# A decoder layer on one core: half of a gated mixer one product earlier, constants behind the input on another queue, row vectors in high and low parts

## The chip, the cores and the metric

The kernel runs on one core of one Trainium2 chip. A core has TensorE (PE, matrix products), VectorE (DVE), ScalarE (ACT), GpSimd (POOL), and SyncE (SP), which here only issues DMAs. Times are microseconds (us) of the device for one execution; the number that counts is the median over runs of the same kernel. [...]

## The reference

One decoder layer on a sequence of 1024 tokens of width 1024, fp32:

```python
proj = x @ w_in + b_in
u, v, c_q, c_kv, k_rope_raw, gate_gm, gate_mla = jnp.split(proj, IN_SPLITS, axis=-1)
y_gm = gmlp_branch(gelu(u), gelu(v), gm_ln_g, gm_ln_b, gm_w_s, gm_b_s) @ w_gm_out   # u * (tril(W_s) LN(v)_chunk + b)
y_mla = mla_branch(c_q, c_kv, k_rope_raw, positions, ...) @ w_mla_out                # 16 heads, causal
merged = sigmoid(gate_gm) * y_gm + sigmoid(gate_mla) * y_mla
x = layer_norm(DEEPNORM_ALPHA * x + merged @ w_o, ln1_g, ln1_b)
x = layer_norm(DEEPNORM_ALPHA * x + memory_cross_attention(x, mem, w_mq, w_mk, w_mv, w_mo), ln2_g, ln2_b)
y_moe = hierarchical_moe(x, ...)                                                     # top-1 group, top-2 experts
return layer_norm(DEEPNORM_ALPHA * x + y_moe, ln3_g, ln3_b)
```

The gated mixer (gMLP) works in chunks of 128 tokens with 8 channel groups; the two halves of the sequence (4 chunks each) are computed one after the other. The latent attention (MLA) has 16 heads. The memory attention has 256 memory tokens and 4 heads.

## The kernel before

**Products in three passes.** Every fp32 operand is split into a rounded high part (fp32r) and a remainder (`split`, L108: the high part by ACT, the low part by DVE), and a product is three fp32r matmuls, high by high, high by low and low by high (`mm3`, L125 to L127, and `proj_t`, L380 to L384). A weight tile goes through `load_w` (L114): SP loads it (L118), ACT and DVE split it, PE reads it. There are 3 raw buffers and 5 split ones, so the loads run several products ahead.

**What sets the order.** Outside the hand-ordered stages (the attention sweep, router and experts) the framework's scheduler puts the instructions on each engine in an order that it works out from the program and from tile buffers; the program text decides who waits on whom, and a stage written earlier is usually issued earlier. Each engine then runs its list in order and waits at an instruction whose input is missing. `defer(n, f)` in the program puts an action n products later.

**Start.** `latents` (L220) loads x, transposed, in eight tiles of 128 x 1024 (512 KB each), and the q-latent weights in four. `late_consts` (L205) follows in the text, six small DMAs on SP's queue (biases, norm gains, rope table).

**Input projection.** `proj_in_t` (L311) is one product of x with 128 of the columns: 24 steps of two matmuls of 128 x 512, then ACT's gelu or sigmoid into `to` and a store. Products 8 to 15 are one gate (`gg_d`), 16 to 23 the other (`gm_d`); 0 to 7 are u. v is made by `proj_v` and stored in `v_d`.

**gMLP.** `gmlp(half)` (L674) reads four chunks of v (`vl`, SP L698), normalises each by two DVE instructions (L699, L700) and splits them into `vs`. It returns `step(g)`: one group's product of `wsT` and `vs` (L704, by mm3), ACT's bias, a load of u, and one product later `turn` (L713): PE transposes, DVE multiplies, SP stores `a_d`. There are eight steps per half, two for each product of the loop in `build` (L1710 to L1723). After the last step `load_a` (L737) loads the eight 512 KB tiles of `a_d` into `aT` and splits them.

**Gated product and MLA.** `gate_gm` (L744) makes eight products of `aT` with `w_gmo` (24 steps of two matmuls each) and, between them, runs the first steps of the attention, which loads per head (`load`, L478): `kr_d` and `kn_d` into `kT` (32 and 64 partitions), `qn_d` and `qr_d` into `qT` (64 and twice 16 partitions), `vv_d` into `vT`. `kT`, `qT` and `vT` lie where x's tiles were, so these loads cannot start before x's last product (23) has ended.

**Memory keys.** `mem_kv` (L634) makes eight products (f = 0 to 7), each 24 matmuls of 128 x 256. Beside them `factors` (L762) turns the attention's row sums into factors by way of GpSimd's queue (`sum_d`, `rinv_d`, `fac`), and `scale_o` (L789) spreads them by two matmuls (L798) a tile. `next(scale)` (L658) places the first of them after f = 5 and the second after f = 7.

**Experts and the end.** The expert stage runs in pairs numbered i; PE is its bound and ACT and DVE split the weights (`wh`, `wl`). From i = 20 `final_loads` (L1557) brings the two vectors of the last norm, each of 1024, on one partition, and spreads them over 128 partitions by fp32 matmuls with a row of ones (L1570). `final` (L1573) norms eight tiles of 128 tokens, the last instruction of each an L1623 on DVE for tiles 5 to 7, and stores them (L1624).

Of the kernel before, what the change touches and what calls it, by code (L numbers as in the profile page):

```python
# [13 lines left out]
F32 = mybir.dt.float32  # L14
FR = mybir.dt.float32r
# [3 lines left out]
ALU = mybir.AluOpType  # L19
# [47 lines left out]
ALL = slice(0, 1024)  # L67
# [7 lines left out]
class K:  # L75
# [126 lines left out]
        self.ones = p.tile([128, 128], FR, name="ones")  # L202
        ts(self.ones, jp, 0.0, 1.0, op0=ALU.mult, op1=ALU.add)

    def late_consts(self):  # L205
        self.router_consts()
        for t, n in ((self.bt, "b_t"), (self.gq, "g_q"), (self.gkv, "g_kv"), (self.bs, "b_s"), (self.fr, "rope_c"), (self.rb, "b_r")):
            self.nc.sync.dma_start(t, self.i[n])

    def natural(self, ps, t, x, w, kts=range(8), nk=8):  # L210

# [8 lines left out]
    def latents(self, xT, fill):  # L220

        nc = self.nc
        with ExitStack() as px:
            small = px.enter_context(self.pool("p1small", 2))
            pss = [self.bank() for _ in range(8)]
            wt = None
            for kk in range(4):
                for kt in (2 * kk, 2 * kk + 1):
                    raw = self.gp.tile([128, 1024], F32, name="xraw", tag="g")
                    nc.sync.dma_start(raw, self.i["xT"][kt])  # L230
                    self.split(xT.at(0, kt, ALL), xT.at(1, kt, ALL), raw)
                    if kt % 2 == 0:
                        wt = self.load_w(self.i["w_cq"][kk], 768)
                for kt in (2 * kk, 2 * kk + 1):
                    o = (kt % 2) * 384
                    for t in range(8):
                        self.natural(pss[t][:, :384], t, xT, lambda k: (wt[:, 0, o:o + 384], wt[:, 1, o:o + 384]), [kt])
                    self.unit()
            self.late_consts()
            bcq = small.tile([128, 384], F32, name="bcq", bufs=1)  # L240
            self.bcast(bcq, self.i["b_cq"])
            bkv = small.tile([128, 320], F32, name="bkv", bufs=1)
# [391 lines left out]
    def mem_kv(self, px):  # L634

        nc = self.nc
        mt = [p.tile([128, 2048], FR, name="memT", tag="act").rearrange("p (k n) -> p k n", k=8) for p in self.pa]
        for k in range(2):
            self.split(mt[0][:, 4 * k:4 * k + 4], mt[1][:, 4 * k:4 * k + 4], self.memr[:, k])
        px.close()  # L640
        self.oT = Act(self.pb, "oT")
        fac = self.factors(px)
        next(fac)
        scale = self.scale_o()
        for f in range(8):
            w = self.load_w(self.i["w_mk"][f], 1024)
            ps = self.bank()
            for kt in range(8):
                self.mm3(ps[:, :256], *w128(w)(kt), mt[0][:, kt], mt[1][:, kt], kt == 0, kt == 7)
            st = self.gp.tile([128, 1024], F32, name="mkst", tag="g").rearrange("p (a n) -> p a n", a=4)  # L650
            self.split(st[:, 0].bitcast(FR), st[:, 1], ps[:, :256])
            self.unit()
            self.defer(1, lambda f=f, st=st: nc.sync.dma_start(self.mk_d[f], st[:, 0:2]))
            self.load_o(f)
            if f == 0:
                next(fac, None)
            if f in (5, 7):
                next(scale)  # L658
        for sl in range(2):
            wts = [self.load_w(self.i["w_mv"][sl, kk], 1024) for kk in range(4)]  # L660
            for m in range(2):
                ps = self.bank()
                ms = slice(m * 128, (m + 1) * 128)
                for kt in range(8):
                    self.mm3(ps, mt[0][:, kt, ms], mt[1][:, kt, ms], *w512(wts)(kt), kt == 0, kt == 7)
                st = self.gp.tile([128, 1024], F32, name="mvst", tag="g").rearrange("p (a n) -> p a n", a=2)
                self.split(st[:, 0].bitcast(FR), st[:, 1], ps)
                self.unit()
                self.defer(1, lambda m=m, sl=sl, st=st: nc.sync.dma_start(self.mv_d[m, :, :, sl * 512:(sl + 1) * 512], st))
                next(scale)  # L670
        for _ in scale:
            pass
# [774 lines left out]
    def experts(self, rest, xg):  # L1447
        nc, tc = self.nc, self.tc
# [8 lines left out]
        for i in range(NP):  # L1457
# [33 lines left out]
                sel = self.select(gi[:, NP - 1:])  # L1491
            if i == 24:
                self.nb = nc.values_load(self.nbi[0:1, 0:1], min_val=0, max_val=15)
            if i in (22, 24):
                next(lgb, None)
            if i == NP - 1:
                self.flush()
# [59 lines left out]
    def final_loads(self, px):  # L1557
        nc = self.nc
        self.lgb = px.enter_context(self.pool("lgb", side="right")).tile([128, 2, 1024], F32, name="lgb")
        self.fin = px.enter_context(self.pool("fins", 8, side="right"))  # L1560
        one = self.fin.tile([1, 128], F32, name="one", bufs=1)
        nc.gpsimd.memset(one, 1.0)
        for j, n in enumerate(("ln3_g", "ln3_b")):
            row = self.fin.tile([1, 1024], F32, name="row", bufs=1)
            nc.sync.dma_start(row, self.i[n])
            yield
            for q in range(2):
                c = slice(q * 512, (q + 1) * 512)
                pg = self.bank_g()
                nc.tensor.matmul(pg, one, row[:, c], start=True, stop=True)  # L1570
                nc.scalar.activation(self.lgb[:, j, c], pg, AF.Copy)  # L1571

    def final(self, first=True):  # L1573

        nc, mm = self.nc, self.nc.tensor.matmul
# [15 lines left out]
        def row_sum(t):  # L1591
# [27 lines left out]
            if t < 5:  # L1619
                nc.scalar.activation(u, u, AF.Copy, scale=r)  # L1620
                nc.gpsimd.tensor_tensor(u, u, lb, op=ALU.add)
            else:
                stt(u, u, r, lb, op0=ALU.mult, op1=ALU.add)  # L1623
            nc.sync.dma_start(self.out[t], u)  # L1624

        rows = [row_sum(t) for t in range(8)]
        for t in range(9):
# [16 lines left out]
def build(nc, tc, ctx, ins, out, upto=99):  # L1644
# [25 lines left out]
    with ExitStack() as dense:  # L1670
# [5 lines left out]
        with ExitStack() as late, ExitStack() as mla, ExitStack() as front:  # L1676
                k.psp = front.enter_context(k.pool("psd1", 8, PSUM))
                with ExitStack() as px:
# [19 lines left out]
                    with ExitStack() as gm:  # L1698
                        k.g1 = gm.enter_context(k.pool("g1"))
                        k.gsm = gm.enter_context(k.pool("gsm", 2))  # L1700
                        k.proj_v(xT)
                        k.proj_in_t(xT, 8)
                        st = k.gmlp(0)
                        k.proj_in_t(xT, 9)
                        k.proj_in_t(xT, 10)
                        for j in range(4):
                            st(2 * j)
                            k.proj_in_t(xT, 11 + j)
                            st(2 * j + 1)
                        k.proj_in_t(xT, 15)  # L1710
                        st = k.gmlp(1)
                        k.proj_in_t(xT, 16)
                        k.proj_in_t(xT, 17)
                        for j in range(4):
                            st(2 * j)
                            k.proj_in_t(xT, 18 + j)
                            st(2 * j + 1)
                        k.proj_in_t(xT, 22)
                        k.flush()
                    w = k.load_w(k.i["w_t"][23], 1024)  # L1720
                    aT = Act(front.enter_context(k.pool("aT", 8, side="right")), "aT")
                    k.load_a(aT)
                    k.proj_in_t(xT, 23, w)  # L1723
                    k.flush()
                k.mem_load(late)
                k.mla_pools(mla)
# [50 lines left out]
    n = 0  # L1777
# [128 lines left out]
```

## Time and profile before

| | |
|---|---|
| median of 3 runs | 2033.64 us (2032.84 to 2034.22) |
| the profiled execution's own time | 2035.97 us |
| its span | 2034.2 us |
| mean granted clock of TensorE | 0.985 |
| PE busy | 1977.6 us, 97% of the span |
| DVE busy | 1292.5 us, 64% |
| ACT busy | 1003.3 us, 49% |
| POOL busy | 449.2 us, 22% |
| chain that ended last | PE 91%, DMA 3%, DVE 3%, ACT 1%, issue 1% |
| DMA | 457.29 MB, mean 225 GB/s |

PE's share of busy time counts a matmul at the low clock as busy for twice as long, so time is lost in two ways: PE idle, and PE busy at a granted clock of 0.50. A row of the timeline gives start, duration, engine, line, operation, tiles and, in brackets, the idle time just before it and what ended that. A row of a DMA issue (SPq) says when SP issued it and how long that took, not when the data landed.

### The profile page before, as it was taken

The page shows a single profiled execution, that of the slowest core. Times are in us where ns is not written, and L with a number is a line of the kernel's source. Part 1 is how long each engine was busy: PE and PEld are TensorE (multiplying, and loading weights), DVE is VectorE, ACT ScalarE, POOL GpSimd, SP SyncE. Part 2 cuts the span into 40 slices and gives each one's busy share as a digit, 9 for nine tenths or more (in the row PEclk, how much of TensorE's full clock was granted, in tenths as well). Part 3 has the DMA queues.
Part 4 walks back from the last instruction along what each step waited for, and adds up shares of the span by engine and source line. Part 5 has one row for each costly group of instructions (what it writes and reads, how often), then busy time and mean ns, then how long its engine had stood idle before and what let it go on. Part 6 is the DMA issues. An engine that isn't in the chain of part 4 may idle for free.

```text
span 2034.2 us, 25602 instructions
## 1 busy us (share of the span) xinstructions
PE 1977.6 (97%) x9468; PEld 1630.4 (80%) x9468; DVE 1292.5 (64%) x2040; ACT 1003.3 (49%) x1267; POOL 449.2 (22%) x243
## 2 busy tenths in 40 slices
PE   8999999999999999999999999997999999999996
PEld 8888888888787777777888888886788888888884
DVE  5636533441335888857436516477888888888887
ACT  4432422322304777764212315233777777777774
POOL 0002000000100111110001100022545555557752
PEclk9999999999999999999999999997999999999998
DMA  5154963353783555537535712555899999999966
GB/s 184 54 210 155 382 196 134 143 189 136 245 251 104 126 125 125 125 133 239 184 106 180 268 62 73 161 218 231 286 372 381 381 387 396 401 392 369 377 260 250
DMA packets 147897, 457.29 MB, mean 225 GB/s; under 512 B 18077, under 2 KB 64029, under 8 KB 118744
## 3 DMA queue, kind: packets, MB, share of 16 engines
q1 hardware_dynamic: 138040, 438.58, 61.7%
q0 software_dynamic: 9728, 17.03, 2.2%
q8 instruction: 76, 1.25, 0.2%
q14 instruction: 53, 0.43, 0.1%
HBM read 367.10 MB, written 104.79 MB: 232 GB/s over the span
## 4 chain that ended last, share of the span: by engine, by line
PE 91%; DMA 3%; DVE 3%; ACT 1%; issue 1%; SPq 0%; POOL 0%; POOLq 0%; ACTq 0%
PE bank L125 9%; PE bank L126 9%; PE bank L127 9%; PE py L1355 8%; PE bank L380 8%; PE bank L382 8%; PE bank L384 8%; PE pg L125 6%; PE pg L127 5%; PE pg L126 5%; PE po L564 2%; PE po L566 2%; PE po L565 2%; PE st L538 1%; PE st L540 1%; PE st L542 1%
## 5 line engine op out<-in xcount | busy, mean ns | idle before, releaser
L1426 ACT ACTIVATE wh<-raw 128x2048 fp32r<-128x2048 f32 (+1 forms) x198 | 361.1, 1859 | 36.3 <-issue 31.4
L1435 DVE TENSOR_TENSOR wl<-raw,wh 128x2048 fp32r<-128x2048 f32 (+1 forms) x166 | 363.3, 2236 | 4.6 <-PE pg L126 3.0
L1435 POOL TENSOR_TENSOR wl<-raw,wh 128x2048 fp32r<-128x2048 f32 x32 | 202.9, 6340 | 227.6 <-ACT wh L1426 227.6
L110 ACT ACTIVATE wsp<-wraw 128x1024 fp32r<-128x1024 f32 (+5 forms) x118 | 111.6, 947 | 263.7 <-PE bank L384 155.2
L125 PE MATMUL pg<-wh,ex 128*128 128x512 f32 x512 | 203.4, 397 | 0.7 <-ACT ex L110 0.7
L126 PE MATMUL pg<-wl,ex 128*128 128x512 f32 x512 | 200.0, 391 | 2.0 <-DVE wl L1435 2.0
L127 PE MATMUL pg<-wh,ex 128*128 128x512 f32 x512 | 200.6, 392 | 0.0
L111 DVE TENSOR_TENSOR wsp<-wraw,wsp 128x1024 fp32r<-128x1024 f32 (+5 forms) x118 | 127.6, 1083 | 96.2 <-ACT wsp L110 93.7
L1355 PE MATMUL py<-wh,ehs 128*128 128x512 f32 x512 | 143.7, 402 | 2.9 <-DVE ehs L111 2.4
L380 PE MATMUL bank<-xT,wsp 128*128 128x512 f32 x384 | 120.1, 390 | 0.0
L382 PE MATMUL bank<-xT,wsp 128*128 128x512 f32 x384 | 119.9, 390 | 0.0
L384 PE MATMUL bank<-xT,wsp 128*128 128x512 f32 x384 | 119.7, 390 | 0.0
L735 POOL TENSOR_TENSOR xr<-xr,lb 128x1024 f32<-128x1024 f32 x12 | 28.7, 2395 | 409.4 <-ACT xr L734 409.4
L546 ACT ACTIVATE pe<-st 128x768 f32<-128x768 f32 (+5 forms) x128 | 86.3, 674 | 59.6 <-DVE st L544 59.5
L126 PEld LDWEIGHTS pg<-wl,ex 128*128 128x128 f32 x512 | 96.7, 189 | 21.3 <-DVE wl L1435 2.3
L125 PEld LDWEIGHTS pg<-wh,ex 128*128 128x128 f32 x512 | 96.4, 188 | 21.1 <-ACT lgb L1571 1.5
L127 PEld LDWEIGHTS pg<-wh,ex 128*128 128x128 f32 x512 | 96.5, 189 | 20.6
L1355 PEld LDWEIGHTS py<-wh,ehs 128*128 128x128 f32 x512 | 91.3, 189 | 19.4 <-DVE ehs L111 3.1
L125 PE MATMUL bank<-wsp,xT 128*128 128x512 f32 (+2 forms) x256 | 91.2, 363 | 6.5 <-ACT wsp L110 6.5
L319 ACT ACTIVATE to<-bank,cols 128x512 f32<-128x512 f32 x48 | 30.4, 684 | 133.7 <-PE bank L384 133.7
L548 ACT ACTIVATE pq<-pe 128x768 fp32r<-128x768 f32 (+5 forms) x128 | 91.3, 713 | 4.1
L126 PE MATMUL bank<-wsp,xT 128*128 128x512 f32 (+2 forms) x256 | 91.6, 358 | 0.0
(410 smaller groups left out, 4627.4 us busy)
## 6 DMA issues: line engine op xcount, KB each, us to landing
raw<-w_gu SPq DMA_DIRECT2D x124, 1024.0 KB
raw<-w_dn SPq DMA_DIRECT2D x62, 1024.0 KB
wraw<-w_t SPq DMA_DIRECT2D x24, 512.0 KB
kn_d<-st SPq DMA_DIRECT2D x8, 1024.0 KB
qn_d<-st SPq DMA_DIRECT2D x8, 1024.0 KB
vv_d<-vt SPq DMA_DIRECT2D x16, 512.0 KB
qT<-qn_d SPq DMA_DIRECT2D x16, 512.0 KB
kT<-kn_d SPq DMA_DIRECT2D x16, 512.0 KB
```

The lines of the kernel that those rows point to most:

```text
L110: a = nc.scalar.activation(hi, src, AF.Copy)
L111: (lo_eng or nc.vector).tensor_tensor(lo, src, hi.bitcast(F32), op=ALU.subtract)
L125: mm(out, ah, bh, start=start, stop=False)
L126: mm(out, ah, bl, start=False, stop=False)
L127: mm(out, al, bh, start=False, stop=stop)
L380: mm(ps, wh, x.at(0, kt, h), start=st, stop=False)
L382: mm(ps, wh, x.at(1, kt, h), start=False, stop=False)
L384: mm(ps, wl, x.at(0, kt, h), start=False, stop=sp)
L548: nc.scalar.activation(pq[:, 0, q0:], e[:, q0:], AF.Copy)
L1355: self.nc.tensor.matmul(py[:, q * 512:(q + 1) * 512], hs[:, a, js], w[b][:, j * 1024 + q * 512:j * 1024 + (q + 1) * 512], start=start and ...
L1426: self.nc.scalar.activation(w[0][:, c], self.raws[n][:, c], AF.Copy)
L1435: eng.tensor_tensor(w[1][:, c], self.raws[n][:, c], w[0][:, c].bitcast(F32), op=ALU.subtract)
```

## The change

The change has six parts.

- **Start.** The first x tile and the first weight tile are loaded and split in two halves each (512 and 384 columns), in turn. The six constants are issued by GpSimd instead of SP, and wait there for the ACT instruction that splits the last x tile.
- **gMLP.** `gmlp(1)` is called ahead of product 15 instead of behind it, and its steps stand one product earlier: the first two around product 17 instead of 18.
- **aT.** With that `load_a` stands ahead of product 22 instead of 23.
- **Memory keys.** The first `next(scale)` comes after f = 6 instead of f = 5.
- **Last norm's vectors.** They are loaded in four pieces of 512 straight into row 0 of their final tile, split into high and low on one partition, and spread by two fp32r matmuls each with ones; the pieces are worked on in pairs 21 to 28 instead of 22 and 24.
- **End.** The last L1623 and its store go in two halves of 512 columns.

```diff
-    def late_consts(self):
+    def late_consts(self, behind):
         self.router_consts()
         for t, n in ((self.bt, "b_t"), (self.gq, "g_q"), (self.gkv, "g_kv"), (self.bs, "b_s"), (self.fr, "rope_c"), (self.rb, "b_r")):
-            self.nc.sync.dma_start(t, self.i[n])
+            d = self.nc.gpsimd.dma_start(t, self.i[n])
+            self.tc.add_manual_dep(d.ins, behind.ins.name, mybir.DependencyInfo(mybir.DependencyClass.Sync, mybir.DependencyReason.DATA), reason="behind larger transfers")
...
+                    if kt == 0:
+                        wraw = self.rawp.tile([128, 1024], F32, name="wraw", tag="wraw")
+                        wt = self.wp.tile([128, 2, 1024], FR, name="wsp", tag="wsp")
+                        cs = [(slice(512 * j, 512 * j + 512), slice(384 * j, 384 * j + 384)) for j in range(2)]
+                        for c, cw in cs:
+                            nc.sync.dma_start(raw[:, c], self.i["xT"][kt][:, c])
+                            nc.sync.dma_start(wraw[:, cw], self.i["w_cq"][kk][:, cw])
+                        for c, cw in cs:
+                            self.split(xT.at(0, kt, c), xT.at(1, kt, c), raw[:, c])
+                            self.split(wt[:, 0, cw], wt[:, 1, cw], wraw[:, cw])
+                        continue
...
-            if f in (5, 7):
+            if f in (6, 7):
                 next(scale)
...
-            if i in (22, 24):
+            if 21 <= i <= 28:
                 next(lgb, None)
...
-        one = self.fin.tile([1, 128], F32, name="one", bufs=1)
-        nc.gpsimd.memset(one, 1.0)
         for j, n in enumerate(("ln3_g", "ln3_b")):
-            row = self.fin.tile([1, 1024], F32, name="row", bufs=1)
-            nc.sync.dma_start(row, self.i[n])
-            yield
             for q in range(2):
                 c = slice(q * 512, (q + 1) * 512)
+                high, low = (self.fin.tile([1, 512], FR, name=m, bufs=1) for m in ("high", "low"))
+                row = self.lgb[:1, j, c]
+                nc.sync.dma_start(row, self.i[n][:, c])
+                yield
+                self.split(high, low, row)
+                yield
                 pg = self.bank_g()
-                nc.tensor.matmul(pg, one, row[:, c], start=True, stop=True)
+                nc.tensor.matmul(pg, self.ones[:1], high, start=True, stop=False)
+                nc.tensor.matmul(pg, self.ones[:1], low, start=False, stop=True)
                 nc.scalar.activation(self.lgb[:, j, c], pg, AF.Copy)
...
-                stt(u, u, r, lb, op0=ALU.mult, op1=ALU.add)
-            nc.sync.dma_start(self.out[t], u)
+                for c in halves if t == 7 else [slice(0, 1024)]:
+                    stt(u[:, c], u[:, c], r, lb[:, c], op0=ALU.mult, op1=ALU.add)
+                    if t == 7:
+                        nc.sync.dma_start(self.out[t][:, c], u[:, c])
+            if t < 7:
+                nc.sync.dma_start(self.out[t], u)
...
+                        st = k.gmlp(1)
                         k.proj_in_t(xT, 15)
-                        st = k.gmlp(1)
                         k.proj_in_t(xT, 16)
-                        k.proj_in_t(xT, 17)
                         for j in range(4):
                             st(2 * j)
-                            k.proj_in_t(xT, 18 + j)
+                            k.proj_in_t(xT, 17 + j)
                             st(2 * j + 1)
-                        k.proj_in_t(xT, 22)
+                        k.proj_in_t(xT, 21)
                         k.flush()
-                    w = k.load_w(k.i["w_t"][23], 1024)
+                    w = k.load_w(k.i["w_t"][22], 1024)
                     aT = Act(front.enter_context(k.pool("aT", 8, side="right")), "aT")
                     k.load_a(aT)
-                    k.proj_in_t(xT, 23, w)
+                    k.proj_in_t(xT, 22, w)
+                    k.proj_in_t(xT, 23)
                     k.flush()
```

Line numbers behind the start grow by 12 to 14 with the change (L741 becomes L755, L489 becomes L503, L322 becomes L336).

On SP's list, at the end of the gMLP in the kernel before, the eight loads of `aT` follow the last store of the mixer (`a_d`) and the last gate weight, and the attention's first loads (`kT`, `qT`, L482 to L489) stand soon behind them:

```order
156 L718 DMA a_d<-ul 128x512
157 L118 DMA wraw<-w_gmo 128x1024
158 L741 DMA aT_3897<-a_d 128x1024
165 L741 DMA aT_3904<-a_d 128x1024
166 L753 DMA gt<-gg_d 128x1024
167 L482 DMA kT_4004<-kr_d 32x2048
168 L485 DMA qT_4008<-qn_d 64x2048
170 L322 DMA gm_d<-to 128x1024
172 L489 DMA kT_4004<-kn_d 64x2048
```

The same place on SP's list in the changed kernel:

```order
151 L732 DMA a_d<-ul 128x512
152 L118 DMA wraw<-w_gmo 128x1024
153 L755 DMA aT_3844<-a_d 128x1024
160 L755 DMA aT_3851<-a_d 128x1024
161 L336 DMA gm_d<-to 128x1024
162 L118 DMA wraw<-w_gmo 128x1024
163 L767 DMA gt<-gg_d 128x1024
164 L496 DMA kT_4010<-kr_d 32x2048
165 L499 DMA qT_4014<-qn_d 64x2048
166 L336 DMA gm_d<-to 128x1024
168 L503 DMA kT_4010<-kn_d 64x2048
```

Between the `aT` loads and the attention's loads there now stand one more gate store and one more weight, those of a whole product.

On PE's list, around the memory keys in the kernel before, the two L798 matmuls stand behind the sixth product (each product is 24 rows of L125, L126, L127), and the seventh and eighth follow:

```order
3345 L126 MATMUL bank<-memT,wsp 128x256
3346 L127 MATMUL bank<-memT,wsp 128x256
3347 L798 MATMUL bank<-fac,fsel 128x512 x2
3348 L125 MATMUL bank<-memT,wsp 128x256
3349 L126 MATMUL bank<-memT,wsp 128x256
3396 L798 MATMUL bank<-fac,fsel 128x512 x2
```

In the changed kernel the same two matmuls, now L812, stand behind the seventh product, and the next two behind the eighth:

```order
3367 L126 MATMUL bank<-memT,wsp 128x256
3368 L127 MATMUL bank<-memT,wsp 128x256
3369 L812 MATMUL bank<-fac,fsel 128x512 x2
3370 L125 MATMUL bank<-memT,wsp 128x256
3371 L126 MATMUL bank<-memT,wsp 128x256
3394 L812 MATMUL bank<-fac,fsel 128x512 x2
```

One product of 24 matmuls has moved ahead of the first scaling; the second scaling keeps its place.

## Rows read from the trace of the kernel before

**Rows 1.** Three stretches: length, busy per engine (instructions), PEclk, DMA share, GB/s.
```profile
3.50:4.00 0.50, 0.00 (x0) 0.00 (x0) 0.00 (x0) 0.00 (x0) 0.00 (x0) 1.00 0.98 395
780.80:789.80 9.00, 8.82 (x44) 6.61 (x42) 7.61 (x23) 7.10 (x9) 1.34 (x2) 1.00 0.97 187
1807.36:1827.24 19.88, 19.88 (x91) 15.29 (x89) 15.15 (x11) 14.72 (x13) 13.56 (x6) 1.00 1.00 396
```

**Rows 2.** Timeline of ACT, start.
```profile
4.69 1.06 ACT L110 ACTIVATE xT<-xraw 128x1024 fp32r<-128x1024 f32 x1 [2.63 <-DMA xraw<-xT]
5.65 0.83 ACT L110 ACTIVATE wsp<-wraw 128x768 fp32r<-128x768 f32 x1
...
22.87 1.06 ACT L110 ACTIVATE xT<-xraw 128x1024 fp32r<-128x1024 f32 x1 [0.29 <-DMA xraw<-xT]
...
50.02 1.84 ACT L264 ACTIVATE cqT<-bank,cols 128x512 fp32r<-128x512 f32 x3 [3.12 <-PE bank L262]
```

**Rows 3.** Timeline of PE, start.
```profile
6.53 2.93 PE L125 MATMUL bank<-wsp,xT 128*128 128x384 f32 x8 [6.53 <-ACT wsp L110]
...
11.82 0.36 PE L126 MATMUL bank<-wsp,xT 128*128 128x384 f32 x1
```

**Rows 4.** Timeline of POOL, memory keys: the load of the factors.
```profile
913.98 0.52 POOL L783 DMA_DIRECT2D fac<-rinv_d  x1 [5.41 <-DMA rinv_d<-rs]
```

**Rows 5.** Timeline of DVE, norm and splits of v.
```profile
443.16 2.48 DVE L699 SCALAR_TENSOR_TENSOR vl<-vl,vmv,vlg 128x1024 f32<-128x1024 f32 x2
...
458.48 1.22 DVE L111 TENSOR_TENSOR vs<-vl,vs 128x1024 fp32r<-128x1024 f32 x1 [1.13 <-ACT vs L110]
```

**Rows 6.** Timeline of PE, first step of the second half.
```profile
462.06 0.39 PE L125 MATMUL bank<-vs,wsT 128*128 128x512 f32 x1
```

**Rows 7.** Timeline of SP, from the last mixer store to the first keys.
```profile
529.17 3.83 SPq L741 DMA_DIRECT2D aT<-a_d  x8
...
536.84 0.32 SPq L482 DMA_DIRECT2D kT<-kr_d  x1
...
541.17 0.47 SPq L489 DMA_DIRECT2D kT<-kn_d  x1
```

**Rows 8.** Timeline of PE, first gated product and first keys.
```profile
541.94 0.73 PE L382 MATMUL bank<-aT,wsp 128*128 128x512 f32 x2 [0.59 <-DVE aT L111]
...
547.96 0.61 PE L384 MATMUL bank<-aT,wsp 128*128 128x512 f32 x2
552.98 0.76 PE L506 MATMUL bank<-kT,qT 96*128 96x256 f32 x2 [4.41 <-DMA kT<-kn_d]
...
558.37 0.62 PE L380 MATMUL bank<-aT,wsp 128*128 128x512 f32 x2
```

**Rows 9.** Timeline of SP, a later head's loads.
```profile
780.29 0.44 SPq L485 DMA_DIRECT2D qT<-qn_d  x1
```

**Rows 10.** Timeline of PE, that head's first use of its keys.
```profile
790.03 0.36 PE L506 MATMUL pm<-kT,qT 96*128 96x256 f32 x1 [0.41 <-DMA kT<-kn_d]
```

**Rows 11.** Timeline of PE, memory keys.
```profile
917.11 0.28 PE L126 MATMUL bank<-memT,wsp 128*128 128x256 f32 x1
917.23 0.28 PE L127 MATMUL bank<-memT,wsp 128*128 128x256 f32 x1
919.77 1.21 PE L798 MATMUL bank<-fac,fsel 32*128 32x512 f32 x2 [2.26 <-DMA fac<-rinv_d]
...
926.75 0.28 PE L125 MATMUL bank<-memT,wsp 128*128 128x256 f32 x1
```

**Rows 12.** Chain of waits, experts: start, us, what.
```profile
1813.95 1.91 PE pg L1570 x4
1815.86 0.43 PE pg L125
1816.29 0.23 PE pg L126
```

**Rows 13.** Timeline of DVE, end.
```profile
2027.71 1.29 DVE L1623 SCALAR_TENSOR_TENSOR raw<-raw,rs,lgb 128x1024 f32<-128x1024 f32 x1
```

More of the change, by code (lines that the diff above doesn't have):

```diff
@@ L229, in latents @@
                     raw = self.gp.tile([128, 1024], F32, name="xraw", tag="g")
+                    if kt == 0:
[9 more added lines that the diff above has]
+                        continue
                     nc.sync.dma_start(raw, self.i["xT"][kt])
-                    self.split(xT.at(0, kt, ALL), xT.at(1, kt, ALL), raw)
+                    self.last = self.split(xT.at(0, kt, ALL), xT.at(1, kt, ALL), raw)
                     if kt % 2 == 0:
@@ L238, in latents @@
                     self.unit()
-            self.late_consts()
+            self.late_consts(self.last)
             bcq = small.tile([128, 384], F32, name="bcq", bufs=1)
```

## The prediction

> **What bounds the kernel now.** I read four views in this order. First the busy times by engine: PE works nearly throughout, so a wait of PE is paid one for one, and work of the other engines costs nothing until PE waits for it. Next the list of what PE waited for, which is short; three entries stand out that the change touches, the start, the first keys of the attention and the factors of the memory stage. [...] Last the timelines of SP, DVE, ACT and POOL ahead of those places, for what the waiting instruction stood behind. The sum goes place by place. A product of x is 24 pairs of matmuls; thirteen pairs take 6.02 us (541.94 to 547.96 in [rows 8]), so a product is about 11.0 us.
>
> **Start.** The first matmul stands at 6.53 and waits for ACT's split of the first weight tile [rows 3]. ACT begins the split of x at 4.69, when its 512 KB have landed, and that of the weights at 5.65 (0.83 us) [rows 2]. With halves, 256 KB less stand ahead of the first split: at 395 GB/s [rows 1] 0.65 us, so it begins at 4.05; the half weight tile (192 KB) lands 0.5 later, at 4.55. A split of 1024 columns takes 1.06 and one of 768 takes 0.83, so I put 512 at 0.60 and 384 at 0.48: x to 4.6, weights to 5.1, first matmul at 5.1 to 5.2. Everything behind moves with it, the low clock until 11.82 [rows 3] too: gain 1.4. The ends are 0 (both halves land as late as the whole) and 2.4 (data and splits both at half of their time). The trace shows 395 GB/s with several transfers in flight, none waiting for another to end. [...]
>
> The six constants go to GpSimd's queue and wait there for the last split of x, which ends at 23.9 [rows 2]. Issues of 0.52 us each as for `fac`, and its landing by 919.77, 5.8 us after the issue [rows 4, 11], put them in place by 33. The first reader shown is ACT at 50.02 [rows 2], so 16 us cover this. Behind the waiting DMAs GpSimd has only the rope tables' work, which needs one of these constants in any case. If the cover went, each us of lateness would be a us of PE.
>
> **gMLP's second half.** PE meets the first step at 462.06 [rows 6]; one product earlier that is 451.1. The norm and splits of v run on DVE from 443.16 to 459.7 (458.48 + 1.22) [rows 5], so if they began when they do now, PE would wait 8.6. But the loads of v move too, in front of the preceding gate store and weight on SP, and DVE may write `vs` once PE has read the first half's from it, two products (22 us) ahead of this step, at about 429. The 16.5 us from there end at 445.6, five us ahead of PE: cost 0, with 8.6 and a clock fall as the other end.
>
> **aT and the first keys.** The eight `aT` loads are issued at 529.17, and PE waits 0.59 for their split at 541.94. PE's last pair of that product, as long as the others, ends at 548.4; then it waits for `kT` until 552.98, 4.6 us with the step to it, and has the low clock to about 558.3 [rows 7, 8]; 5.3 us at half speed lose 2.6. Together 7.8. One product earlier the loads start at 518.2 and their 4 MB are in before 531, so the 0.59 goes, and SP's queue is free when x's last product ends at about 536.7. What stays is that `kT` lies in x's place: its first load is issued at 536.84 [rows 7] and not sooner. Up to the last key then come `kr_d` (256 KB), `qn_d` (512), a gate store (512), `qr_d` (256) and `kn_d` (512). For a later head, issue of `qn_d` at 780.29 to first use of the keys at 790.03 is 9.7 us for the same three loads [rows 9, 10]; `kr_d` at the 187 GB/s of that stretch adds 1.4 and the store at 395 GB/s 1.3 [rows 1]. That gives 549.2, against 547.8 when PE comes. From bytes alone, 1.57 MB at 187 and the store, it would be 546.5, no wait; if the keys landed as now, PE would wait 5.1 and the whole term would be 0. I take the sum of the rows: a wait of 1.4. After 0.59 of idling the clock stayed, after 2.26 it fell [rows 8, 11]; 1.4 is half way, so I charge half of the 2.6: gain 7.8 - 1.4 - 1.3 = 5.1.
>
> [...]
>
> **Memory keys.** PE ends the sixth product at 917.35 (its matmuls start 0.12 apart), waits until 919.77 for `fac`, and has the low clock until 926.75 [rows 11]: 2.3, and 6.6 us at half speed, 3.2 more; 5.5 in all. A further product ahead of it is 24 such matmuls, 2.9 us: PE arrives at 920.2, half a us behind `fac`, whose chain (POOL, DVE, ACT) hangs on the attention's end and not on these products. The seventh product's weights are split before PE needs them now, since PE stands still here. Gain 5.5; if another reason lowers the clock here anyway, 2.3, and if the chain slips by 1 us, half a us less.
>
> **Last norm's vectors.** Two fp32 pieces take 1.91, and the next step 0.43 in place of 0.23 [rows 12]: 2.1 a vector, 4.2 in all. Four times two matmuls at 0.23 with the same step behind them are 4 x (0.46 + 0.20) = 2.6: gain 1.6 (0 to 2.4). The splits are on one partition, but as long as 512 columns: 0.6 on ACT (as above) and about 0.65 on DVE (half of 1.22 [rows 5] and a little). In such a pair of 19.88 us PE is busy throughout and DVE and ACT for 15.15 and 14.72 [rows 1]: 4.7 and 5.2 us hide it.
>
> **End.** Today the last DVE instruction runs 2027.71 to 2029.0 [rows 13], and its 512 KB leave after that. With halves 256 KB follow the last instruction: at 395 GB/s 0.65 less, minus the second half's own start-up of 0.1: gain 0.5 (0 to 0.7).
>
> **Sum.** 1.4 + 0 + 5.1 + 5.5 + 1.6 + 0.5 = 14.1 us, off the profiled execution's own 2035.97 (span 2034.2): 2021.9. That execution lies 2.3 above the median of the runs, so I forecast 2019.5.
>
> **Rivals.**
> *The keys stay as late as they are.* x's last product releases their place at the same time as before, and the slow loads alone make PE wait; the term of 5.1 is 0, the rest stays: 2024.6. For it speaks that the last key is issued behind four other transfers; against it, that the 4 MB of `aT` no longer run beside them. 0.18.
> *No wait for the keys at all.* They land by 546.5 as the bytes say; the term is 7.8 and the time 2016.8. For it: 187 GB/s was measured while other transfers shared the queue; against it, the measured 9.7 us. 0.17.
> *v comes too late.* If the loads of v find no free buffer and start when they do now (DVE from 443.16), PE waits 8.6 and loses 2.6 by the clock: 14.1 - 11.2 = 2.9 gained, 2030.7. Against it, SP's new order. 0.05.
> *The weight feed breaks in the experts, and the kernel is slower.* ACT's and DVE's extra splits (1.25 us together) stand between weight splits of four pairs. Should PE have no slack there, each piece would stall it in its pair and once more in the next one, each time 1.25 and a clock fall of 3.3 as in the memory stage: 8 x 4.55 = 36.4 against 14.1, 2055.9. It turns the sign from 3.5 us per piece. PE has no wait inside the pair shown, and the idle 4.7 us speak against it. 0.03.
>
> **How the numbers follow.** My own case holds 0.57, with 2016.5 to 2022.5 as its range (start and end at their bounds, clock fallen or not). Taking in the two rivals for the keys gives 2014 to 2026. About 0.2% (4 us) is what a measurement of this kernel tells from no change: below 2029.6 lie my case and the first two rivals, 0.92; within lies the third, 0.05; above lies the fourth, 0.03.
>
> **What will show it.** In the new profile: the first matmul at about 5.1; no wait for `aT`, its loads issued near 518 less the start's gain; a wait of 0 to 3 us at L520 for `kT`, where 4.4 stood, and a granted clock that stays at 1.00 or falls once; no wait at L812, and 1.00 behind it; four pieces of about 0.66 in the experts, with no wait for `wl` or `wh` in pairs 21 to 28; and a last store of 256 KB. The forecast is wrong if PE waits at the second half's first gMLP step, if `kT` lands no earlier relative to PE, or if the clock falls at places where it does not now.

## The result, and the profile after

The changed kernel takes 2020.47 us (median of 4 runs, 2018.15 to 2021.94), against 2033.93 for the kernel before (4 runs). The ratio is 0.9932 with a 95% interval of 0.9915 to 0.9949, 13.5 us less. On another chip it came out at 0.9939 (0.9926 to 0.9953). The forecast was 2019.5, in a range of 2014 to 2026.

The profiled execution takes 2019.54 us with a span of 2017.8, so 16.4 us lie between the two spans. First, the changed kernel's list of what PE waited for, in us in total, times, longest:

```profile
PE bank L125 <- ACT wsp L110: 4.9, 1, 4.9
PE pg L1101 <- DVE M L1099: 3.8, 1, 3.8
PE py L1369 <- DVE ehs L111: 2.4, 1, 2.4
PE pg L126 <- DVE wl L1449: 2.2, 1, 2.2
...
PE pm L520 <- DMA kT<-kn_d: 2.0, 5, 0.8
PE bank L125 <- ACT memT L110: 1.6, 1, 1.6
```

The first keys' wait (4.41 in [rows 8]) and the factors' wait (2.26 in [rows 11]) are off the list, and the start's entry is 1.6 shorter ([rows 3]: 6.53). The entries of the router, `wl` and `ehs` are as they were, within 0.2. The keys of later heads (L520) are waited for a little longer: 2.0 in five waits, where the trace before has 0.6 in two.

At the start, the timelines of ACT and of PE, where [rows 2, 3] had 4.69, 5.65, 6.53 and 11.82:

```profile
3.79 0.63 ACT L110 ACTIVATE xT<-xraw 128x512 fp32r<-128x512 f32 x1 [1.73 <-DMA xraw<-xT]
4.33 0.51 ACT L110 ACTIVATE wsp<-wraw 128x384 fp32r<-128x384 f32 x1
```

```profile
4.89 1.65 PE L125 MATMUL bank<-wsp,xT 128*128 128x384 f32 x4 [4.89 <-ACT wsp L110]
...
8.89 0.35 PE L125 MATMUL bank<-wsp,xT 128*128 128x384 f32 x1
```

The half tile is there 0.90 sooner than the whole one, the split of the weights' half begins 1.3 sooner, and the first matmul stands 1.64 sooner. From 4.0 us after it on, at 8.89, the matmuls of 384 columns start about 0.17 us apart instead of 0.32; in the trace before, this step came 5.3 us behind the first matmul, at 11.82. PEclk, by the profile the share of its full speed that TensorE was granted, reads 1.00 on both sides of the step in both traces.

At the end of x's products, the timelines of SP and of PE, where [rows 7, 8] had the loads of `aT` at 529.17, the wait for `aT` of 0.59 and the one for `kT` of 4.41:

```profile
516.04 4.17 SPq L755 DMA_DIRECT2D aT<-a_d  x8
...
534.58 0.33 SPq L496 DMA_DIRECT2D kT<-kr_d  x1
...
537.60 1.14 SPq L503 DMA_DIRECT2D kT<-kn_d  x1
```

```profile
534.39 0.62 PE L394 MATMUL bank<-aT,wsp 128*128 128x512 f32 x2
...
545.66 0.48 PE L520 MATMUL bank<-kT,qT 96*128 96x256 f32 x2 [0.23 <-issue]
545.98 0.63 PE L394 MATMUL bank<-aT,wsp 128*128 128x512 f32 x2
```

The keys' first load is still issued only when x's last product has ended, as forecast; but from there to their first use are 11.1 us (534.58 to 545.66), not 16.1 (536.84 to 552.98 [rows 7, 8]). PE hardly stops. The stretch behind it, by window (length, busy of PE, PEld, DVE, ACT, POOL, PEclk, DMA share, GB/s), is at the full clock:

```profile
546.20:550.20 4.00, 4.00 (x19) 3.31 (x18) 2.09 (x7) 0.33 (x1) 0.00 (x0) 1.00 1.06 326
```

In the gMLP, DVE's last split of v and PE's first step, against 459.7 and 462.06 [rows 5, 6]:

```profile
443.19 1.23 DVE L111 TENSOR_TENSOR vs<-vl,vs 128x1024 fp32r<-128x1024 f32 x1
```

```profile
448.92 0.39 PE L125 MATMUL bank<-vs,wsT 128*128 128x512 f32 x1
```

No wait, and 4.5 us in hand. The constants' six issues on GpSimd run from 22.76 to 26.28, behind the last split of x; nobody waits for one. In the memory stage PE meets the scaling without a wait (timeline of PE; [rows 11] had it at 919.77 behind 2.26 of idling, and at the low clock):

```profile
910.97 0.73 PE L812 MATMUL bank<-fac,fsel 32*128 32x512 f32 x2
```

In the experts, the chain of waits at one piece of the last norm's vectors (start, us, what):

```profile
1799.24 0.42 PE pg L1585
1799.67 0.23 PE pg L1586
1799.89 0.43 PE pg L125
```

Both the first matmul of the piece and the first one behind it take 0.2 more than the 0.23 of the others ([rows 12] showed the second of these, behind the fp32 matmuls). A piece costs 0.42 + 0.23 + 0.20 = 0.85 and its pair is 18.61 long, 0.88 more than the 17.73 of a pair without.

Between the two traces the time goes like this. By the first `aT` matmul (536.65 to 534.39) 2.3 us are gained, 1.6 by the first matmul and 0.6 by the earlier step to the closer spacing. Behind the first keys it is 9.65 (558.37 to 548.72), so the keys gave 7.4. The attention gave back 0.45. Up to the last scaling it is 14.7 (955.9 to 941.2): the factors gave 5.5. A fall of the clock at 1234 in the trace before has no counterpart, and one at 1456 in the trace after has none in the other; they cancel to 0.1. The vectors gave 0.8 and the end 0.9.

The fall at 1456 is one of the signs that I had named as making the forecast wrong, the clock falling where it did not before. The wait ahead of it is not new:

```profile
1454.62 0.73 PE L1369 MATMUL py<-wh,ehs 128*128 128x512 f32 x2 [2.42 <-DVE ehs L111]
```

This wait of 2.42 stands in all fourteen traces of this document, the two of the kernel before among them, and the clock fell behind it in this one alone.

### The profile page after: what moved, and what is told of

The parts are those of the page before. It is cut to its first block, busy times and chain, and to the rows that moved or that the text cites. A ratio compares the mean times of both kernels' runs of the same rounds, so it can differ in the third digit from the quotient of the medians.

```text
span 2017.8 us, 25627 instructions
## 1 busy us (share of the span) xinstructions
PE 1969.8 (98%) x9468; PEld 1624.0 (80%) x9468; DVE 1292.9 (64%) x2047; ACT 1005.4 (50%) x1273; POOL 468.0 (23%) x248
## 4 chain that ended last, share of the span: by engine, by line
PE 92%; DVE 3%; DMA 2%; issue 1%; ACT 1%; SPq 0%; POOL 0%; DVEq 0%; POOLq 0%; ACTq 0%
PE bank L125 9%; PE bank L126 9%; PE bank L127 9%; PE py L1369 9%; PE bank L394 8%; PE bank L396 8%; PE bank L398 8%; PE pg L125 6%; PE pg L127 6%; PE pg L126 6%; DMA kT<-kn_d 2%; PE po L578 2%; PE po L580 1%; PE po L579 1%; PE px L1331 1%; PE st L552 1%
## 5 line engine op out<-in xcount | busy, mean ns | idle before, releaser
L125 PE MATMUL pg<-wh,ex 128*128 128x512 f32 x512 | 203.4, 397 | 0.7 <-ACT ex L110 0.7
L126 PE MATMUL pg<-wl,ex 128*128 128x512 f32 x512 | 199.9, 390 | 2.2 <-DVE wl L1449 2.2
L127 PE MATMUL pg<-wh,ex 128*128 128x512 f32 x512 | 200.6, 392 | 0.0
L126 PEld LDWEIGHTS pg<-wl,ex 128*128 128x128 f32 x512 | 96.6, 189 | 21.5 <-DVE wl L1449 2.5
L125 PEld LDWEIGHTS pg<-wh,ex 128*128 128x128 f32 x512 | 96.4, 188 | 21.0 <-issue 1.4
L127 PEld LDWEIGHTS pg<-wh,ex 128*128 128x128 f32 x512 | 96.4, 188 | 20.6
L125 PE MATMUL bank<-wsp,xT 128*128 128x512 f32 (+2 forms) x256 | 91.3, 360 | 4.9 <-ACT wsp L110 4.9
L126 PE MATMUL bank<-wsp,xT 128*128 128x512 f32 (+2 forms) x256 | 91.5, 358 | 0.0
```

What stands on the lines that cost most here:

```text
L125: mm(out, ah, bh, start=start, stop=False)
L126: mm(out, ah, bl, start=False, stop=False)
L127: mm(out, al, bh, start=False, stop=stop)
```

## Experiments

Each kernel's time is given as a ratio to the kernel before on the same chip. Single executions of one kernel spread over 4 to 10 us here, so ratios carry intervals of about 0.1%, and what lies below that is read from the traces, from one fixed instruction to another.

**gmlp_only**: the kernel before, with the gMLP half and `aT` one product earlier and nothing else.

```diff
+                        st = k.gmlp(1)
                         k.proj_in_t(xT, 15)
-                        st = k.gmlp(1)
...
-                    w = k.load_w(k.i["w_t"][23], 1024)
+                    w = k.load_w(k.i["w_t"][22], 1024)
```

> Before with only the gMLP half and the aT loads one product earlier. In the changed kernel the distance to before grew from 2.3 us at x's last product to 9.7 us in the second gated product, 7.4 us. Theory (the aT loads no longer run ahead of the first keys, so the keys land in time): this part alone gives 7 to 7.6 us, median about 2026.4; no wait for kT above 0.5 us at the first keys and a granted clock of 1.00 from 540 to 560. Rival (part of it came from the start's shift or from the constants' new queue): 5 us or less, with a kT wait of 1 to 3 us left.

Measured: 0.9959 (0.9946 to 0.9972), 8.3 us less. PE's timeline at the first keys, and the window behind them:

```profile
548.66 0.48 PE L506 MATMUL bank<-kT,qT 96*128 96x256 f32 x2 [1.21 <-DMA kT<-kn_d]
```

```profile
549.00:553.00 4.00, 4.00 (x20) 3.32 (x19) 1.84 (x6) 0.00 (x0) 0.00 (x0) 1.00 1.10 337
```

Neither side is met exactly: the wait is 1.2, near my forecast's 1.4, but the clock stays. From the first `aT` matmul to the seventh pair of the next product this kernel takes 15.3 us, the kernel before 21.7, the changed kernel 14.3. So this part alone gives 6.4 here; the eight traces with the early `aT` take 14.3 to 15.6, so the last us varies from run to run.

**late_aT**: the changed kernel with the `aT` loads held back by a product; with them `load_a` stands behind product 22 again in the program, and the gMLP steps stay early.

```diff
-            self.nc.sync.dma_start(a, self.a_d[f])
+            d = self.nc.sync.dma_start(a, self.a_d[f])
+            self.tc.add_manual_dep(d.ins, self.act.ins.name, ..., reason="one product later")   # act: last ACT instruction of product 22
...
+                        k.proj_in_t(xT, 22)
                         k.flush()
-                    w = k.load_w(k.i["w_t"][22], 1024)
+                    w = k.load_w(k.i["w_t"][23], 1024)
...
-                    k.proj_in_t(xT, 22, w)
-                    k.proj_in_t(xT, 23)
+                    k.proj_in_t(xT, 23, w)
```

> The changed kernel with the aT loads tied behind ACT's last instruction of product 22, so that they are issued about one product later, near where they stood before, while the gMLP steps stay early. Theory (the 4 MB of aT in SP's queues ahead of the first keys make the wait): PE waits for aT by about 0.6 us and for kT by 3 to 5 us at the first keys, the clock falls behind it, 6 to 8 us slower than the changed kernel, about 2027 to 2028. Rival (the keys are bound by x's last product alone): the kT wait stays under 1.3 us and the time within 2 us of the changed kernel.

Measured: 0.9972 (0.9961 to 0.9983), 2029.6 against 2023.4 for the changed kernel on the same chip, 6.2 us slower. SP's and PE's timelines:

```profile
525.03 4.81 SPq L755 DMA_DIRECT2D aT<-a_d  x8
...
534.46 0.33 SPq L496 DMA_DIRECT2D kT<-kr_d  x1
...
538.56 0.47 SPq L503 DMA_DIRECT2D kT<-kn_d  x1
```

```profile
551.98 0.77 PE L520 MATMUL bank<-kT,qT 96*128 96x256 f32 x2 [6.67 <-DMA kT<-kn_d]
```

The keys are issued as in the changed kernel (534.46 and 538.56 against 534.58 and 537.60), yet PE gets them at 551.98, 17.5 us behind the first issue instead of 11.1, and waits 6.7. There was no wait for `aT`, where 0.6 was expected. The theory's cause is shown: with the gMLP steps early, the 4 MB of `aT` shortly ahead of the keys bring the wait back. One weight tile and one gate tile stand between the two (issued at 529.94 and 531.04), but the changed kernel has both there too (528.21 and 528.59). The wait is larger than the 3 to 5 expected, and larger than the kernel before's 4.4; no run shows why.

**scale_only**: the kernel before with `if f in (6, 7)` in place of `(5, 7)`. **scale_back**: the changed kernel with `(5, 7)`.

> Before with only the first scaling of the memory stage behind f = 6 instead of 5. Theory (fac's chain is fixed by the attention's end, one product of 2.9 us covers it): no wait for fac and a granted clock of 1.00 behind it, 5.5 us gained, about 2028.4. Rival (the margin of 0.5 us fails or the clock falls there anyway): 2 to 3.5 us gained, about 2031.

> The changed kernel with the first scaling back behind f = 5. So far kernels with the old place show a fac wait of 2.2 to 2.9 us, and from the first memory matmul to the last scaling they took 55.05 to 58.07 us, against 52.5 to 53.3 with the new place. Theory (the wait is certain, the clock fall behind it is not): a fac wait of 2.2 to 2.9, a stretch of 55 to 58, 2 to 5.5 us slower than the changed kernel, 2023 to 2028. Rival (the wait is a matter of the earlier stages, which the change moved too): a wait below 1 us and a stretch below 54.

Measured: scale_only 0.9978 (0.9969 to 0.9987), 4.5 us less, between the theory's 5.5 and the rival's 2 to 3.5; scale_back 0.9953 (0.9936 to 0.9971), against 0.9932 and 0.9939 for the changed kernel on two other chips, 3 to 4 us more, though the intervals overlap. PE at the scaling, in scale_only and in scale_back:

```profile
922.60 0.73 PE L798 MATMUL bank<-fac,fsel 32*128 32x512 f32 x2 [0.56 <-DMA fac<-rinv_d]
```

```profile
914.85 0.79 PE L812 MATMUL bank<-fac,fsel 32*128 32x512 f32 x1 [2.30 <-DMA fac<-rinv_d]
```

scale_only has 0.56 us of waiting for `fac`, where the sum had half a us in hand; in the eight traces with the new place the wait is 0 to 1.1, so that margin is about zero from run to run. The clock behind it is 1.00 in scale_only. In scale_back the wait is back and the clock falls. So the long wait belongs to the place of the scaling and to nothing the other parts moved: the traces show it, the times alone would not.

**before_again**: the kernel before once more, for a second trace.

> The kernel before once more, for a second trace of it: what in its first trace belongs to the kernel and what to one execution. Theory: first matmul 6.0 to 6.6, a kT wait of 4 to 5 and a fac wait of 2 to 3 again; the granted clock behind fac and at 1231, and the us between the first matmul and the clock's rise, may differ. Rival: all of the first trace's low clock stretches come back at the same places.

Measured: 2032.1 us; first matmul at 6.10, the first keys' wait 4.21, the factors' 2.83. The three windows of 3 us that begin 1 us behind the scaling's first matmul, in the kernel before, in this second trace of it, and in scale_back:

```profile
920.77:923.77 3.00, 3.00 (x14) 2.87 (x14) 2.09 (x3) 0.88 (x1) 0.00 (x0) 0.50 0.95 303
```

```profile
921.50:924.50 3.00, 3.00 (x28) 3.00 (x27) 2.42 (x3) 0.52 (x2) 0.00 (x0) 1.00 0.76 230
```

```profile
915.85:918.85 3.00, 3.00 (x14) 2.86 (x14) 2.42 (x3) 0.51 (x2) 0.00 (x0) 0.50 1.00 320
```

In the kernel before, a wait at the same place has 14 matmuls behind it in 3 us in one trace and 28 in the other (2.26 and 2.83 us of waiting). The wait is the kernel's; the fall of the clock behind it comes in some executions and not in others. The fall at 1234 did not come back in this trace, but it did in scale_only (1231.5) and scale_back (1228.6), each time some 178 us ahead of the experts' first px group. In these three the slowest of the 64 matmuls on `e` there takes 417 to 421 ns, and so it does in both_quarters (421), while the ten other traces have 327 to 331: four of fourteen, with the old and the new form alike.

**start_only**: the kernel before with the halves and the constants' new queue. **consts_sp**: the changed kernel with the constants back on SP.

```diff
-            d = self.nc.gpsimd.dma_start(t, self.i[n])
-            self.tc.add_manual_dep(d.ins, behind.ins.name, ...)
+            self.nc.sync.dma_start(t, self.i[n])
```

> Before with only the start: first x and weight tile in halves, constants on GpSimd's queue. Theory (as in the changed kernel, the first matmul moves by 1.6 us and the clock's rise by 2.9, so the low stretch is 0.6 us cheaper too): 2.3 us gained up to x's last product (its first aT matmul at 534.4), median about 2031.4. Rival (only the first matmul counts): 1.6 us, first aT matmul at 535.0. The kT wait of about 4.4 and the fac wait of 2.3 stay in both.

> The changed kernel with the six constants back on SP's queue, the halves kept. Theory (the halves alone move the start): first matmul at 4.7 to 4.9 and x's last product ending as in the changed kernel, 534.4, within 0.5. Rival (the constants' issues on SP delay x's later tiles and PE waits for them in the first products): PE waits of over 0.5 us between 5 and 40 us, x's last product 0.5 to 2 us later.

Measured: start_only 0.9990 (0.9981 to 0.9999), 2.0 us less, first matmul at 4.71, first `aT` matmul at 533.90. consts_sp: 2023.4 in its one execution, first matmul at 4.84, no PE wait between 5 and 40 us; its first `aT` matmul, which follows x's last product, is at 535.25. That is 0.35 beyond the theory's bound, but within what the changed kernel itself shows (534.39 and 535.46). The constants' queue makes no difference that these runs can tell. The extra 0.6 of the ledger is no gain of the change: from the first matmul to the closer spacing the traces show 3.4 to 5.9 us, with either start (5.3, 5.3, 5.9, 3.4, 5.0 for whole tiles; 4.0, 5.9, 3.4, 4.0, 3.7, 5.9, 5.0 for halves).

**start_quarters**: the changed kernel with the first x tile in four pieces, one ahead of the weights' first half.

```diff
-                        cs = [(slice(512 * j, 512 * j + 512), slice(384 * j, 384 * j + 384)) for j in range(2)]
+                        xs, ws = [slice(256 * j, 256 * j + 256) for j in range(4)], [slice(384 * j, 384 * j + 384) for j in range(2)]
+                        order = [(0, xs[0]), (1, ws[0]), (0, xs[1]), (0, xs[2]), (0, xs[3]), (1, ws[1])]   # 0: x, 1: weights
```

> The changed kernel with the first x tile in quarters, one quarter ahead of the first half of the weights. Theory (bytes ahead of the first weights set the first matmul): 128 KB less at 395 GB/s, 0.3 us, so a first matmul at 4.4 to 4.6 where the kernels with halves have it at 4.71 to 5.10. Rival (a transfer's own fixed time sets it): 4.7 to 5.1, no change, and the rest of x comes later.

Measured: first matmul at 4.33, a little below the theory's 4.4 to 4.6. The bytes ahead of it count, and the shorter split of x too (0.42, where halves took 0.63). ACT's timeline:

```profile
3.03 0.42 ACT L110 ACTIVATE xT<-xraw 128x256 fp32r<-128x256 f32 x1 [0.97 <-DMA xraw<-xT]
3.76 0.52 ACT L110 ACTIVATE wsp<-wraw 128x384 fp32r<-128x384 f32 x1 [0.31 <-DMA wraw<-w_cq]
```

Its one execution took 2026.0; in it a wait of 2.4 us for `ehs` in the experts came twice instead of once, far from the edit. Its L1371 matmuls on `ehs` took 405 ns in the mean, as in the changed kernel's trace with the fall at 1456, and 402 in the other twelve traces, so the clock seems to have fallen behind the second. What caused the second wait stays open.

**end_only**: the kernel before with the vectors in high and low parts and the last store in halves.

```diff
-                nc.tensor.matmul(pg, one, row[:, c], start=True, stop=True)
+                nc.tensor.matmul(pg, self.ones[:1], high, start=True, stop=False)
+                nc.tensor.matmul(pg, self.ones[:1], low, start=False, stop=True)
```

> Before with only the last norm's vectors as high and low parts and the last store in halves. Theory (from the changed kernel's pairs: a piece costs 0.88 us, four of them 3.5, against twice 2.14): 0.8 us from the vectors and 0.9 at the end, 1.7 in all, median about 2032.2. Rival (my forecast's sizes): 1.6 and 0.5, 2.1 in all; told apart by the pairs' length in the trace, 18.61 by the theory and 18.39 by the rival.

Measured: 0.9987 (0.9977 to 0.9997), 2.6 us less. A pair with a piece is 18.61 long, the theory's figure, by the px groups at both of its ends in the chain:

```profile
1806.02 0.87 PE px L1317 x8
...
1824.63 0.87 PE px L1317 x8
```

From the last matmul of the px group of the last pair but one to the end of the span are 79.5 us, against 80.1 before: 0.6, not the 0.9 of the theory.

**mem_quarters**: the changed kernel with the memory tokens split in four pieces. **both_quarters**: that and start_quarters together. **after_again**: the changed kernel, their partner.

```diff
-        for k in range(2):
-            self.split(mt[0][:, 4 * k:4 * k + 4], mt[1][:, 4 * k:4 * k + 4], self.memr[:, k])
+        for k in range(4):
+            ks, r = slice(2 * k, 2 * k + 2), 2 * (k % 2)
+            self.split(mt[0][:, ks], mt[1][:, ks], self.memr[:, k // 2, r:r + 2])
```

> The changed kernel with the memory tokens split in four pieces of 512 columns instead of two of 1024 at the head of the memory stage, where PE waits 1.63 us for ACT's first piece and 0.40 for DVE's. Theory (the first piece's length is the wait): 1.63 becomes about 1.1 and 0.40 about 0.4, 0.5 us gained, and the low clock behind it stays. Rival (the shorter idle time keeps the clock up): 2.6 us gained, the granted clock at 1.00 through the first product.

> The changed kernel with both refinements, the first x tile and the memory tokens in quarters. Theory (the two small gains of the traces add: first matmul 0.4 to 0.5 sooner, the head of the memory stage 0.8 shorter): 1.2 us under the changed kernel, ratio to before about 0.9930, first matmul at 4.3 to 4.5, 1.2 us idle at the memory stage's first matmul. Rival (the later quarters of x, or the extra splits, cost it again): 0.994 or more.

> The changed kernel itself, on the chip of this call, as the partner of the other three. By the first measurement 0.993 of before; the ledger of the two traces (2.3 start, 7.4 keys, 5.5 factors, 0.8 vectors, 0.9 end, and clock falls at other places that cancel) puts 14 to 17 us between the two.

Measured: 0.9934 (0.9921 to 0.9948), 0.9941 (0.9927 to 0.9955) and 0.9939 (0.9926 to 0.9953). The head of the memory stage in mem_quarters, and in the changed kernel:

```profile
890.04 1.44 PE L125 MATMUL bank<-memT,wsp 128*128 128x256 f32 x5 [1.20 <-ACT memT L110]
```

```profile
888.63 0.86 PE L125 MATMUL bank<-memT,wsp 128*128 128x256 f32 x5 [1.63 <-ACT memT L110]
889.89 0.58 PE L126 MATMUL bank<-memT,wsp 128*128 128x256 f32 x1 [0.40 <-DVE memT L111]
```

The two waits of 2.03 us became one of 1.20, and the clock still fell there, as in every trace. But nothing of that reaches the last scaling: from the beginning of these waits to it are 54.4 and 54.5 us in mem_quarters and both_quarters, and 54.2 to 54.9 (mean 54.5) in the six other traces with the new place of the scaling. In mem_quarters the low clock lasts longer, to about 896.1, 6.1 us behind the first matmul, where the changed kernel's trace has 4.4; in both_quarters PE, which comes sooner, waits for the factors again:

```profile
913.95 0.73 PE L815 MATMUL bank<-fac,fsel 32*128 32x512 f32 x2 [1.11 <-DMA fac<-rinv_d]
```

The 0.9941 of both_quarters lies where its rival stood (0.994 or more), not at the theory's 0.9930. Neither refinement can be told from the changed kernel by its time; no version beats it clearly.

## Why the prediction was right, and where its terms were off

All traces together give a firmer ledger than the two alone. The rows are means over the traces that have the old or the new form of a part, from one fixed instruction to another:

| part | old form, us (traces) | new form, us (traces) | gain | forecast |
|---|---|---|---|---|
| first matmul | 6.21 (5) | 4.86 (7) | 1.4 | 1.4 |
| first `aT` matmul to the 7th pair of the next product | 21.5 (5) | 15.0 (8) | 6.5 | 5.1 |
| first memory matmul to the last scaling | 56.7 (6) | 52.9 (6) | 3.8 | 5.5 |
| experts, first px group to that of the last pair but one | 542.5 (5) | 541.8 (7) | 0.7 | 1.6 |
| that px group to the end | 80.1 (5) | 79.4 (9) | 0.7 | 0.5 |
| sum | | | 13.1 | 14.1 |

The first row leaves out the kernels with a quartered start, the second late_aT, and the third the two kernels with quartered memory tokens. The experts' row leaves out two traces of the new form with a disturbance of their own: the changed kernel's first (clock fall at 1456) and start_quarters (the second `ehs` wait).

Three stretches lie between the rows. From the first matmul to the first `aT` matmul 0.2 is gained, and from the last scaling to the experts 0.4. From the seventh pair to the memory stage 1.1 is lost (340.9 in five traces, 342.0 in eight): there PE waits for later heads' keys for 1.6 us in the mean with the old form (0.6 to 2.2) and for 3.0 with the new one (2.0 to 4.1). So part of the keys' gain seems to be paid back further on, which the prediction had not considered; that the earlier first keys cause the later waits is not shown. With these stretches the sum is 12.6, against the measured 13.5, and 12.4 by the second ratio.

That the forecast came so near is in part luck. Its mechanisms held, but the keys' term was 1.4 too small, the factors' 1.7 and the vectors' 0.9 too large, and the loss among the later heads was missing; these errors leave 1.5 us of the 14.1.

**Start.** Right in mechanism and size. In the traces ACT begins on 128, 256 and 512 KB of x 2.25 (0.78 to 3.03), 3.0 and 3.9 us behind the issue. The two loads ahead of the first matmul run beside one another: issued 0.45 apart (0.78 and 1.23), their splits began 0.54 apart (3.79 and 4.33), and with quarters both came sooner still (3.03 and 3.76). What I called the low clock until 11.82 is the matmuls' wider spacing; PEclk reads 1.00 there.

**gMLP and constants.** Right: no wait for either, and 4.5 us in hand for v.

**First keys.** The mechanism was right, including that the keys' own loads start no earlier against x's last product; late_aT shows the cause. The term was too small by 1.4, for two reasons. The wait left over is 0.2 to 1.5 us in eight traces where I had the sum of two rows, 1.4; and I charged half a clock fall, which came in none of them. Five of the traces have less than 1.0 us of waiting, so my second rival, no wait at all, was as near as my own case.

**Factors.** The step was right; the gain was overstated by 1.7. The 2.26 of waiting is certain, 2.2 to 2.9 in six traces, but I added 3.2 us of low clock as if it belonged to the wait. Behind 2.25, 2.26 and 2.30 us of waiting the clock fell, behind 2.93 it fell too, 1.6 us later, and behind 2.65 and 2.83 it stayed. In these six traces the length of the wait does not decide it. (The 6.6 us of low clock in that term is a misreading as well: from 919.77 to 926.75 are 7.0.) A fall read from one trace should have been priced as a chance, between 2.3 and 5.5, which I had only as a range.

**Vectors.** The mis-sized term: I priced a piece at 0.66 and it costs 0.88, because the 0.2 that I put behind the piece is also paid ahead of it. The splits are covered, as forecast: PE has no wait in the pairs with a piece, and the slower rival did not come about.

**End.** Right, and slightly larger: with halves the 256 KB leave 4.2 us ahead of the end of the span (2013.64 to 2017.8), before it was 5.2 (2029.0 to 2034.2). DVE's last instructions, the two halves, in the changed kernel:

```profile
2012.22 1.42 DVE L1640 SCALAR_TENSOR_TENSOR raw<-raw,rs,lgb 128x512 f32<-128x512 f32 x2
```

## What to carry to other kernels

A load that waits for a buffer can still be made earlier without touching the buffer: take away what stands in the queues in front of it, here 4 MB that were needed anyway and could be issued one product sooner (16.1 us from the keys' first issue to their first use became 11.1). A gain at one wait can be paid back at a later one: the quartered memory tokens shortened a wait by 0.8, and none of it reached the last scaling. A wait seen in a trace is the kernel's, but a fall of TensorE's clock behind it is partly that execution's (at the factors it came in four of six traces); price the wait fully and the fall as a chance, and take a second trace of the same kernel before believing in it. When several small edits go in together, read each from one fixed instruction to another, since the median cannot tell 1 us.

## What the runs showed of the hardware

- At the start, matmuls of 384 columns were 0.32 us apart at first; the step to 0.17 came 3.4 to 5.9 us behind the first matmul in the twelve traces with whole or half tiles: 2.5 us of spread, by an estimate worth 1.2 us, half of it. The changed kernel alone showed 4.0 and 5.9. PEclk reads 1.00 there in all ten of these traces that have windows of it.
- A wait of 2.25 to 2.30 us was followed by a granted clock of 0.50 in three traces, while 2.65 and 2.83 us in the same place were not. How often the clock falls differs by place: behind a wait of 4.2 to 6.7 us at the first keys in six of six traces, at the head of the memory stage in fourteen of fourteen, behind the 2.42 us for `ehs` in one of fourteen.
- The same key loads took 11.1 us from first issue to first use with 1 MB issued 6 us ahead of them, and 17.5 us with 4 MB more issued some 5 to 9 us ahead, though SP had issued them just as early.
- Two fp32r matmuls from a single partition cost 0.88 us between full ones that take 0.23 each: 0.2 of it ahead of them and 0.2 behind.
